# Moving the norm's sums and the first scalings of an MLP one loop step later

## The chip, the cores and the metric

The kernel runs on one core of one Trainium2 chip. The metric is the device time of one execution in microseconds; of several runs the median counts. Engines are named as in the profile: PE (matmuls), DVE (vector), ACT (activations), POOL (GpSimd), SP (the queue from which the DMAs are issued).

## The reference

Two layers on a sequence of 1024 tokens with 1024 features: a recurrent block, then chunked band attention, and behind each of them an MLP with its own RMS norm. Only the MLPs are touched by the change:

```python
def rmsnorm(x, g):
    xf = x.astype(jnp.float32)
    y = xf * lax.rsqrt(jnp.mean(xf * xf, axis=-1, keepdims=True) + EPS)
    return (y * g.astype(jnp.float32)).astype(x.dtype)

def sqrelu_mlp(x, w_up, w_down):
    return jnp.square(jax.nn.relu(x @ w_up)) @ w_down
...
        h = h + sqrelu_mlp(rmsnorm(h, mlp_norm[l]), w_up[l], w_down[l])
```

The factor of the norm is one number for each token. It is the same for all features, so it can be multiplied in after the product with `w_up`, and this is what the kernel does.

## The kernel before

Activations lie transposed: 128 features on the partitions, 512 tokens (a "half" h of the sequence) in the free dimension. Every fp32 operand is split in two fp32r tiles (`wh`, `wl` for weights, `h`, `l` for data: ACT makes the high part with a copy, DVE the low part with a subtraction), and one product of two blocks is three matmuls, high x high, high x low, low x high (lines 334 to 336).

`w_up` is multiplied by a 2x2 block scheme with seven products in place of eight. `mlp_up` runs 16 block pairs q. For each of them SP loads four weight blocks into `raw` tiles (A11, A12, A21, A22), POOL forms four sums of them (`up_sums`, lines 1044 to 1049), and seven splits are made by `wsplit` (ACT L1035, DVE L1036). Each `product` is 12 matmuls. In short, per q:

- z gets product 0 (bank "pj"), v gets product 1 ("sc"); c11 = z + v (ACT L1132, DVE L1133);
- y gets product 4 ("tp"), z gets product 5, w gets product 2 ("tp"), z gets product 6; c12 and c22 are sums of these (L1145 to L1152);
- `relu` scales c11, c12, c22 by the norm's factor R[0] or R[1] (DVE L1116) and squares them (ACT L1117);
- the `tail`, which is emitted one step later, behind the products 0 and 1 of q+1: product 3 goes into z, and c21 is `relu` of z (so that the bank of z is free only after that L1116); seven results go to DRAM (`hid`).

There are two "pj" banks, so that z of q+2 takes the bank of z of q. The first block pair (q = 0) is begun in `up_begin`, with its c11, c12, c22 in tiles of other pools; it ends with the squares of the last four result blocks and their addition to `norm.acc` (L1106, L1107) and with `c22 = z + c22` (L1108).

R comes from `o.r(h)`, that is `rneg`: the sum of squares `acc[h]` is split (`parts`: ACT L359 makes `ah`, DVE L361 makes `al`), summed over partitions by two matmuls with ones (`sums`: L365, L366), and from that ACT makes Ln (L393), Exp (L394) and a Square (L370), and DVE the two steps of a Newton correction (L371, L372). R[0] and R[1] are made once for each MLP.

`mlp_up` and `mlp_down` are recorded in plain program order, and the tile scheduler of the framework then puts the instructions of each engine in a fixed order of its own; the engines run in that order. What is emitted later has a lower priority there.

Of the kernel before, what the change touches and what calls it, by code (L numbers as in the profile page):

```python
# [13 lines left out]
ALU = mybir.AluOpType  # L14
# [143 lines left out]
def tile_yoco_rglru_chunk_attention(  # L158
# [72 lines left out]
    def bank(tag=None):  # L231
        if tag is None:
            tag = ("pj", "tp", "sc", "pj", "tp", "sc", "po", "sc")[ring[0] % 8]
            ring[0] += 1
        return ps1.tile([P, H2], F32, tag=tag, name=nm(tag), bufs=BANKS[tag])
# [6 lines left out]
    def dma(dst, src):  # L242
        ins = nc.sync.dma_start(dst, src)
        if early[0]:
            early[0] -= 1
            tc.keep_in_program_order(ins)
# [84 lines left out]
    def mm(ps, wp_, xp, start, stop, more=False):  # L331

        (wh, wl), (xh, xl) = wp_, xp
        pe.matmul(ps, lhsT=wh, rhs=xh, start=start, stop=False, skip_group_check=more)  # L334
        pe.matmul(ps, lhsT=wh, rhs=xl, start=False, stop=False, skip_group_check=more)  # L335
        pe.matmul(ps, lhsT=wl, rhs=xh, start=False, stop=stop, skip_group_check=more)  # L336
# [64 lines left out]
    R = [None, None]  # L401
# [631 lines left out]
    def wsplit(raw):  # L1033
        wh, wl = wr("wh"), wr("wl")
        act.activation(wh, raw, AF.Copy)  # L1035
        dve.tensor_tensor(wl, raw, wh.bitcast(F32), ALU.subtract)  # L1036
        return blocks4(wh), blocks4(wl)

    def up_weights(layer, q):
        raw = [wload(w_up[layer, q, x]) for x in range(4)]  # L1040
        return raw, (wsplit(raw[A11]), wsplit(raw[A12])), wsplit(raw[A22])
# [21 lines left out]
    def product(o, ps, n, w, start, depth=range(4)):  # L1063
        for i in depth:
            mm(
                ps, (w[0][:, i, :], w[1][:, i, :]), o.XT[n][i],
                start and i == 0, i == 3, not start and len(depth) == 4,
            )
# [42 lines left out]
    def mlp_up(o, layer, begun):  # L1111

        R = []

        def relu(out, src, h, op):
            dve.scalar_tensor_tensor(out, src, 0.0, R[h], op, ALU.mult)  # L1116
            act.activation(out, out, AF.Square)  # L1117

        (z, a22, c11, c12, c22), ahead = begun
        tail = None  # L1120
        for q in range(NQ + 1):
            if 0 < q < NQ:
                if q == 1:
                    raw, (a11, a12) = ahead
                    a22 = wsplit(raw[A22])
                else:
                    raw, (a11, a12), a22 = up_weights(layer, q)
                z, v = bank("pj"), bank("sc")
                product(o, z, 0, a11, True)
                product(o, v, 1, a12, True)  # L1130
                c11 = sf()
                act.activation(c11, z, AF.Copy)  # L1132
                dve.tensor_tensor(c11, v, c11, ALU.add)  # L1133
            if tail is not None:
                tail()
                tail = None
            if q == NQ:
                break
            if q:
                s1, s2 = up_sums(raw)  # L1140
                y = bank("tp")
                product(o, y, 4, s1, True)
                product(o, z, 5, s2, False)
                c12, c22 = sf(), sf()
                act.activation(c22, y, AF.Copy)  # L1145
                dve.tensor_tensor(c12, z, c22, ALU.add)
                s4, s3 = wsplit(raw[A12]), wsplit(raw[A11])
                w = bank("tp")
                product(o, w, 2, s4, True)
                dve.tensor_tensor(c12, w, c12, ALU.add)  # L1150
                product(o, z, 6, s3, False)
                dve.tensor_tensor(c22, z, c22, ALU.add)  # L1152
            else:
                R.extend((o.r(0), o.r(1)))
            relu(c11, c11, 0, ALU.max)
            relu(c12, c12, 1, ALU.max)
            relu(c22, c22, 1, ALU.min)

            def tail(q=q, z=z, a22=a22, c11=c11, c12=c12, c22=c22):
                product(o, z, 3, a22, False)  # L1160
                dma(hid[0, q], c11)
                dma(hid[2, q], c22)
                t1 = sf()
                dve.tensor_tensor(t1, c11, c12, ALU.subtract)
                dma(hid[4, q], t1)
                dve.tensor_tensor(c12, c22, c12, ALU.subtract)
                dma(hid[6, q], c12)
                t2 = sf()
                dve.scalar_tensor_tensor(t2, t1, -1.0, c22, ALU.mult, ALU.subtract)
                dma(hid[5, q], t2)  # L1170
                c21 = sf()
                relu(c21, z, 0, ALU.min)
                dma(hid[1, q], c21)
                t4 = sf()
                dve.scalar_tensor_tensor(t4, t2, -1.0, c21, ALU.mult, ALU.subtract)
                dma(hid[3, q], t4)
# [147 lines left out]
    X, R = o2.XS, o2.rr  # L1324
# [475 lines left out]
```

## Time and profile before

| | us |
|---|---|
| median of 3 runs | 2140.32 (2138.83 to 2141.16) |
| the profiled execution | 2141.76, of which its span is 2140.0 |
| PE busy | 2092.7 (98% of the span) |
| DVE busy | 1544.4 (72%) |
| ACT busy | 1106.4 (52%) |
| POOL busy | 577.2 (27%) |

A start time in the rows below is in us from the begin of the span. The first MLP's up stage starts near 340, the second's near 1535. "Busy" counts from start to end of an instruction, and instructions of one engine overlap a little: PE issues a 512 column matmul every 0.2275 us in full flow while one row lasts 0.39, and DVE and ACT issue every 0.60 and 0.53 us rows that last 0.68 and 0.62.

### The profile page before, as it was taken

What the parts mean: (1) busy time and instruction counts of PE and PEld (TensorE: products, weight loads), DVE (VectorE), ACT (ScalarE), POOL (GpSimd) and SP (SyncE); (2) the same over time, 40 slices, a digit from 0 to 9 for tenths busy, and PEclk for the clock granted to TensorE, in tenths of its full rate; (3) what the DMA queues carried; (4) which work ended last, traced back from release to release, by engine and by line L of the source; (5) the groups of instructions that cost most, each with busy time, mean ns of one, the idle gap of its engine ahead of it and who ended that gap; (6) DMA issues with size and microseconds to landing.
All of it is one profiled execution on the core that took longest, in us unless ns stands there. A gap on an engine that the chain in (4) does not pass through costs nothing.

```text
span 2140.0 us, 29346 instructions
## 1 busy us (share of the span) xinstructions
PE 2092.7 (98%) x9768; PEld 1732.8 (81%) x9768; DVE 1544.4 (72%) x2602; ACT 1106.4 (52%) x1965; POOL 577.2 (27%) x511
## 2 busy tenths in 40 slices
PE   7999899999999999999999999989999999999999
PEld 5788787888888888887888888878778888888887
DVE  7767768877777776747777877767787777777843
ACT  5777645444434544546666666764443444444631
POOL 0123202333310000127666666650133332000000
PEclk8999999999999999999999999999999999999999
DMA  4111334544469784534323332343364444987732
GB/s 139 35 50 50 107 116 153 182 158 153 149 231 314 240 259 131 161 121 109 86 75 97 91 91 83 87 151 123 103 215 148 155 156 170 332 262 242 244 109 94
DMA packets 174296, 319.21 MB, mean 149 GB/s; under 512 B 20544, under 2 KB 22592, under 8 KB 174144
## 3 DMA queue, kind: packets, MB, share of 16 engines
q1 hardware_dynamic: 174144, 317.33, 45.8%
q8 instruction: 77, 1.26, 0.2%
q14 instruction: 75, 0.61, 0.1%
HBM read 219.73 MB, written 78.64 MB: 139 GB/s over the span
## 4 chain that ended last, share of the span: by engine, by line
PE 86%; DVE 6%; ACT 3%; DMA 2%; issue 2%; SPq 1%; POOL 0%; DVEq 0%; POOLq 0%; ACTq 0%
PE pj L334 11%; PE pj L335 11%; PE pj L336 11%; PE tp L334 6%; PE tp L336 6%; PE tp L335 6%; PE sc L336 4%; PE sc L335 4%; PE sc L334 4%; PE p L335 4%; PE p L334 3%; PE p L336 3%; PE tp L1581 2%; PE po L1609 2%; PE po L1608 1%
## 5 line engine op out<-in xcount | busy, mean ns | idle before, releaser
L334 PE MATMUL pj<-h,wh 128*128 128x512 f32 x1198 | 481.5, 402 | 4.9 <-DVE s L1116 3.6
L335 PE MATMUL pj<-l,wh 128*128 128x512 f32 x1198 | 468.0, 391 | 0.7 <-POOL l L1634 0.7
L336 PE MATMUL pj<-h,wl 128*128 128x512 f32 x1198 | 467.9, 391 | 0.2
L1035 ACT ACTIVATE wh<-raw 128x512 fp32r<-128x512 f32 x349 | 219.1, 629 | 317.5 <-PE po L335 68.9
L1036 DVE TENSOR_TENSOR wl<-raw,wh 128x512 fp32r<-128x512 f32 x349 | 269.8, 775 | 100.3 <-ACT wh L1035 96.5
L336 PEld LDWEIGHTS pj<-h,wl 128*128 128x128 f32 x1198 | 225.2, 188 | 49.4 <-DVE wl L1036 1.0
L334 PEld LDWEIGHTS pj<-h,wh 128*128 128x128 f32 x1198 | 225.8, 189 | 48.5 <-DVE s L1116 4.4
L335 PEld LDWEIGHTS pj<-l,wh 128*128 128x128 f32 x1198 | 226.0, 189 | 38.8 <-POOL l L1634 1.4
L334 PE MATMUL tp<-h,wh 128*128 128x512 f32 x569 | 221.5, 389 | 0.0
L335 PE MATMUL tp<-l,wh 128*128 128x512 f32 x569 | 221.4, 389 | 0.0
L336 PE MATMUL tp<-h,wl 128*128 128x512 f32 x569 | 221.4, 389 | 0.0
L348 DVE TENSOR_TENSOR l<-raw,h 128x512 fp32r<-128x512 f32 x224 | 153.6, 692 | 30.1 <-ACT h L347 28.6
L347 ACT ACTIVATE h<-raw 128x512 fp32r<-128x512 f32 x224 | 137.5, 620 | 56.9 <-DMA raw<-hid 34.1
L335 PE MATMUL sc<-l,wh 128*128 128x512 f32 x425 | 165.8, 390 | 0.0
L336 PE MATMUL sc<-h,wl 128*128 128x512 f32 x425 | 165.7, 390 | 0.0
L334 PE MATMUL sc<-h,wh 128*128 128x512 f32 x425 | 165.4, 390 | 0.0
L334 PE MATMUL p<-h,wh 128*128 128x512 f32 x384 | 153.0, 398 | 11.3 <-ACT h L589 6.4
L1117 ACT ACTIVATE s<-s 128x512 f32<-128x512 f32 x125 | 78.4, 629 | 164.6 <-DVE s L1116 164.6
L1044 POOL TENSOR_TENSOR raw<-raw,raw 128x512 f32<-128x512 f32 x30 | 49.7, 1657 | 405.3 <-DVE wl L1036 398.3
L335 PE MATMUL p<-l,wh 128*128 128x512 f32 x384 | 152.5, 397 | 4.9 <-DVE l L592 2.4
L336 PE MATMUL p<-h,wl 128*128 128x512 f32 x384 | 151.3, 394 | 0.0
L334 PEld LDWEIGHTS tp<-h,wh 128*128 128x128 f32 x569 | 106.8, 188 | 22.4 <-ACT h L1632 0.3
(276 smaller groups left out, 4149.9 us busy)
## 6 DMA issues: line engine op xcount, KB each, us to landing
raw<-hid SPq DMA_DIRECT2D x224, 256.0 KB, 3.6
hid<-s SPq DMA_DIRECT2D x221, 256.0 KB, 2.1
raw<-in_w_down SPq DMA_DIRECT2D x192, 256.0 KB, 3.5
raw<-in_w_up SPq DMA_DIRECT2D x128, 256.0 KB, 2.6
s<-in_w_down SPq DMA_DIRECT2D x64, 256.0 KB, 4.3
raw<-in_w_in SPq DMA_DIRECT2D x32, 256.0 KB, 2.7
raw<-in_w_kv SPq DMA_DIRECT2D x32, 256.0 KB, 3.3
od<-ev SPq DMA_DIRECT2D x48, 128.0 KB, 2.2
```

The lines of the kernel that those rows point to most:

```text
L334: pe.matmul(ps, lhsT=wh, rhs=xh, start=start, stop=False, skip_group_check=more)
L335: pe.matmul(ps, lhsT=wh, rhs=xl, start=False, stop=False, skip_group_check=more)
L336: pe.matmul(ps, lhsT=wl, rhs=xh, start=False, stop=stop, skip_group_check=more)
L347: act.activation(h, src, AF.Copy)
L348: dve.tensor_tensor(l, src, h.bitcast(F32), ALU.subtract)
L1035: act.activation(wh, raw, AF.Copy)
L1036: dve.tensor_tensor(wl, raw, wh.bitcast(F32), ALU.subtract)
L1044: pool.tensor_tensor(raw[A11], raw[A11], raw[A21], ALU.add)
L1117: act.activation(out, out, AF.Square)
L1581: pe.transpose(pt[:, g * P : (g + 1) * P], sc[:, (kb - kb0) * P : (kb - kb0 + 1) * P], ident)
L1608: pe.matmul(out, lhsT=st, rhs=ph[:, off : off + wid], start=x == 0 and y == 0, stop=False)
L1609: pe.matmul(out, lhsT=st, rhs=pl[:, off : off + wid], start=False, stop=y == final)
```

## The change

`R.extend((o.r(0), o.r(1)))` and the three `relu` calls on c11, c12 and c22 go from the body of the loop into `tail`, behind its product 3. They are thus emitted one step later: behind the products 0 and 1 of the next q, its c11, and product 3 of the own q. For q = 0 the whole making of R moves with them. No instruction is added or removed on any engine.

```diff
                 product(o, z, 6, s3, False)
                 dve.tensor_tensor(c22, z, c22, ALU.add)
-            else:
-                R.extend((o.r(0), o.r(1)))
-            relu(c11, c11, 0, ALU.max)
-            relu(c12, c12, 1, ALU.max)
-            relu(c22, c22, 1, ALU.min)
 
             def tail(q=q, z=z, a22=a22, c11=c11, c12=c12, c22=c22):
                 product(o, z, 3, a22, False)
+                if not R:
+                    R.extend((o.r(0), o.r(1)))
+                relu(c11, c11, 0, ALU.max)
+                relu(c12, c12, 1, ALU.max)
+                relu(c22, c22, 1, ALU.min)
                 dma(hid[0, q], c11)
```

The order in which the scheduler puts the instructions differs at the head of each of the two up stages only: on PE over some 120 rows, on DVE and ACT over some 45. From the middle of the third block pair on, and everywhere else in the program, the rows stand on every engine as before. Three places matter.

**Place 1, DVE behind L1108** in the first MLP. `al` is the low part of the sum of squares, `wl` with raw_2491, raw_2489, raw_2487, raw_2485 the low parts of q = 1's blocks (A22 plain, then A21+A22, A22 with its sums, A12 with its sums, A11+A21). Before:

```order
L1108 TENSOR_TENSOR raw_2529<-pj_2455,raw_2529 128x512
L361 TENSOR_TENSOR al_2627<-acc_2313,ah_2625 128x512
L1036 TENSOR_TENSOR wl_2659<-raw_2491,wh_2658 128x512
L1036 TENSOR_TENSOR wl_2723<-raw_2489,wh_2722 128x512
L1036 TENSOR_TENSOR wl_2728<-raw_2491,wh_2727 128x512
L1036 TENSOR_TENSOR wl_2762<-raw_2487,wh_2761 128x512
L371 SCALAR_TENSOR_TENSOR s_2634<-po_2624,s_2634 128x512
L361 TENSOR_TENSOR al_2641<-acc_2315,ah_2639 128x512
L372 SCALAR_TENSOR_TENSOR rneg_2631<-s_2634,rneg_2631 128x512
```

Now:

```order
L1108 TENSOR_TENSOR raw_2529<-pj_2455,raw_2529 128x512
L1036 TENSOR_TENSOR wl_2625<-raw_2491,wh_2624 128x512
L361 TENSOR_TENSOR al_2672<-acc_2313,ah_2670 128x512
L1036 TENSOR_TENSOR wl_2723<-raw_2489,wh_2722 128x512
L1133 TENSOR_TENSOR s_2654<-sc_2629,s_2654 128x512
L1036 TENSOR_TENSOR wl_2728<-raw_2491,wh_2727 128x512
L1036 TENSOR_TENSOR wl_2762<-raw_2487,wh_2761 128x512
L1036 TENSOR_TENSOR wl_2766<-raw_2485,wh_2765 128x512
L1036 TENSOR_TENSOR wl_2805<-raw_2796,wh_2804 128x512
L1036 TENSOR_TENSOR wl_2809<-raw_2798,wh_2808 128x512
L371 SCALAR_TENSOR_TENSOR s_2679<-po_2669,s_2679 128x512
L361 TENSOR_TENSOR al_2686<-acc_2315,ah_2684 128x512
```

The split of A22 now stands ahead of `al`; c11 of q = 1 and three more splits (the last two of q = 2) stand ahead of the Newton step L371.

**Place 2, the sums of the second half** in the first MLP, on ACT and on PE. On ACT, `ah` with acc_2315 is the second half's. Before:

```order
L359 ACTIVATE ah_2625<-acc_2313 128x512
L1035 ACTIVATE wh_2722<-raw_2489 128x512
L393 ACTIVATE rneg_2631<-po_2624,eps 128x512
L1035 ACTIVATE wh_2727<-raw_2491 128x512
L394 ACTIVATE rneg_2631<-rneg_2631 128x512
L1035 ACTIVATE wh_2761<-raw_2487 128x512
L370 ACTIVATE s_2634<-rneg_2631 128x512
L359 ACTIVATE ah_2639<-acc_2315 128x512
```

Now:

```order
L359 ACTIVATE ah_2670<-acc_2313 128x512
L1035 ACTIVATE wh_2722<-raw_2489 128x512
L1035 ACTIVATE wh_2727<-raw_2491 128x512
L1035 ACTIVATE wh_2761<-raw_2487 128x512
L1035 ACTIVATE wh_2765<-raw_2485 128x512
L1035 ACTIVATE wh_2804<-raw_2796 128x512
L1035 ACTIVATE wh_2808<-raw_2798 128x512
L393 ACTIVATE rneg_2676<-po_2669,eps 128x512
L394 ACTIVATE rneg_2676<-rneg_2676 128x512
L370 ACTIVATE s_2679<-rneg_2676 128x512
L359 ACTIVATE ah_2684<-acc_2315 128x512
```

Three more splits now stand ahead of the second `ah`. On PE, the first half's sums (po) stood among the last ten matmuls of q = 1's product 1 and now stand behind product 3 of q = 0 (pj_2455); then comes product 5 of q = 1 (pj_2628). The second half's sums (tp_2683) stand behind that and one matmul of q = 2:

```order
L335 MATMUL pj_2628<-l_2524,wh_2727 128x512
L336 MATMUL pj_2628<-h_2523,wl_2728 128x512
L334 MATMUL sc_2817<-h_1994,wh_2808 128x512
L365 MATMUL tp_2683<-ah_2684,onesr 128x512
L334 MATMUL tp_2732<-h_2031,wh_2722 128x512
L335 MATMUL tp_2732<-l_2032,wh_2722 128x512
L336 MATMUL tp_2732<-h_2031,wl_2723 128x512
L366 MATMUL tp_2683<-al_2686,onesr 128x512
```

Before, the second half's L365 stood right behind product 3 of q = 0, 22 rows behind L365 of the first half; now it is 15 behind it, and product 5 has come ahead of the products 4 and 2 of q = 1.

**Place 3, DVE ahead of c21 of q = 0** in the first MLP, L1116 on pj_2455; the first matmul of z of q = 2 waits for that row. Before:

```order
L371 SCALAR_TENSOR_TENSOR s_2648<-tp_2638,s_2648 128x512
L1133 TENSOR_TENSOR s_2688<-sc_2663,s_2688 128x512
L372 SCALAR_TENSOR_TENSOR rneg_2645<-s_2648,rneg_2645 128x512
L1116 SCALAR_TENSOR_TENSOR s_2688<-s_2688,rneg_2631 128x512
L1116 SCALAR_TENSOR_TENSOR raw_2528<-raw_2528,rneg_2645 128x512
L1116 SCALAR_TENSOR_TENSOR raw_2529<-raw_2529,rneg_2645 128x512
L1036 TENSOR_TENSOR wl_2819<-raw_2808,wh_2818 128x512
L1164 TENSOR_TENSOR s_2705<-raw_2527,raw_2528 128x512
L1036 TENSOR_TENSOR wl_2883<-raw_2806,wh_2882 128x512
L1166 TENSOR_TENSOR raw_2528<-raw_2529,raw_2528 128x512
L1169 SCALAR_TENSOR_TENSOR s_2710<-s_2705,raw_2529 128x512
L1116 SCALAR_TENSOR_TENSOR s_2713<-pj_2455,rneg_2631 128x512
```

Now:

```order
L1116 SCALAR_TENSOR_TENSOR s_2654<-s_2654,rneg_2676 128x512
L1036 TENSOR_TENSOR wl_2883<-raw_2800,wh_2882 128x512
L371 SCALAR_TENSOR_TENSOR s_2693<-tp_2683,s_2693 128x512
L372 SCALAR_TENSOR_TENSOR rneg_2690<-s_2693,rneg_2690 128x512
L1036 TENSOR_TENSOR wl_2888<-raw_2802,wh_2887 128x512
L1116 SCALAR_TENSOR_TENSOR raw_2528<-raw_2528,rneg_2690 128x512
L1116 SCALAR_TENSOR_TENSOR raw_2529<-raw_2529,rneg_2690 128x512
L1036 TENSOR_TENSOR wl_2922<-raw_2798,wh_2921 128x512
L1164 TENSOR_TENSOR s_2705<-raw_2527,raw_2528 128x512
L1166 TENSOR_TENSOR raw_2528<-raw_2529,raw_2528 128x512
L1169 SCALAR_TENSOR_TENSOR s_2710<-s_2705,raw_2529 128x512
L1116 SCALAR_TENSOR_TENSOR s_2713<-pj_2455,rneg_2676 128x512
```

Between L1108 and this L1116 stood 23 DVE rows and stand 25 now: two more splits of q = 2 (wl_2888, wl_2922) have come ahead of it. On PE, four more matmuls of q = 2's product 4 have come ahead of the z that waits for it. In the second MLP the same places are changed in nearly the same way, there with two matmuls in place of four.

## Rows read from the trace of the kernel before

**Rows 1.** The page: the span; busy time of each engine; the chain that ended last, by engine.

```profile
span 2140.0 us, 29346 instructions
PE 2092.7 (98%) x9768; PEld 1732.8 (81%) x9768; DVE 1544.4 (72%) x2602; ACT 1106.4 (52%) x1965; POOL 577.2 (27%) x511
...
PE 86%; DVE 6%; ACT 3%; DMA 2%; issue 2%; SPq 1%; POOL 0%; DVEq 0%; POOLq 0%; ACTq 0%
```

**Rows 2.** Busy time of each engine in stretches at the head of the up stage of the first MLP (340 to 380) and of the second (1550 to 1570), with one from the steady part (400 to 440). Columns: stretch, its length, then for each engine busy us and, in brackets, instructions; then the granted clock of PE as a share of full speed, DMA share, GB/s.

```profile
340.00:350.00 10.00, 7.91 (x32) 5.86 (x31) 9.87 (x13) 5.42 (x11) 3.50 (x3) 0.95 0.01 2
350.00:360.00 10.00, 10.00 (x40) 8.07 (x40) 7.29 (x12) 8.30 (x15) 4.77 (x4) 0.88 0.55 180
360.00:370.00 10.00, 8.25 (x37) 6.52 (x36) 10.00 (x13) 4.52 (x9) 4.08 (x3) 1.00 0.77 265
370.00:380.00 10.00, 9.75 (x43) 7.61 (x42) 9.85 (x15) 5.16 (x10) 3.11 (x3) 1.00 0.83 272
400.00:440.00 40.00, 40.00 (x178) 33.13 (x177) 29.35 (x40) 15.60 (x27) 14.79 (x10) 1.00 0.45 151
...
1550.00:1560.00 10.00, 10.00 (x46) 8.29 (x45) 9.35 (x13) 6.29 (x12) 5.51 (x4) 1.00 0.90 292
1560.00:1570.00 10.00, 8.18 (x35) 6.14 (x35) 9.86 (x15) 4.65 (x8) 3.76 (x3) 1.00 0.75 256
```

**Rows 3.** The timeline of PE in the first MLP. Columns: start, duration, engine, line, operation, out<-in, shape, count; in brackets the idle time before the row and what ended it.

```profile
345.54 0.39 PE L334 MATMUL sc<-h,wh 128*128 128x512 f32 x1
347.94 0.50 PE L365 MATMUL po<-ah,onesr 128*128 128x512 f32 x1 [2.01 <-ACT ah L359]
...
350.13 0.63 PE L334 MATMUL sc<-h,wh 128*128 128x512 f32 x1
350.56 0.63 PE L335 MATMUL sc<-l,wh 128*128 128x512 f32 x1
...
354.67 0.39 PE L365 MATMUL tp<-ah,onesr 128*128 128x512 f32 x1
...
366.94 0.39 PE L335 MATMUL tp<-l,wh 128*128 128x512 f32 x1
369.07 0.50 PE L334 MATMUL pj<-h,wh 128*128 128x512 f32 x1 [1.75 <-DVE s L1116]
...
376.07 0.39 PE L336 MATMUL tp<-h,wl 128*128 128x512 f32 x1
376.71 0.50 PE L334 MATMUL pj<-h,wh 128*128 128x512 f32 x1 [0.25 <-DVE s L1152]
```

**Rows 4.** The same view of PE in the second MLP, the rows with idle time before them.

```profile
1541.33 0.50 PE L365 MATMUL po<-ah,onesr 128*128 128x512 f32 x1 [2.02 <-ACT ah L359]
...
1547.91 0.50 PE L365 MATMUL tp<-ah,onesr 128*128 128x512 f32 x1 [1.26 <-ACT ah L359]
...
1562.49 0.50 PE L334 MATMUL pj<-h,wh 128*128 128x512 f32 x1 [1.82 <-DVE s L1116]
```

**Rows 5.** The timeline of DVE in the first MLP (the last row: the second MLP's L1108), same columns.

```profile
347.74 0.68 DVE L1108 TENSOR_TENSOR raw<-pj,raw 128x512 f32<-128x512 f32 x1
348.35 0.67 DVE L361 TENSOR_TENSOR al<-acc,ah 128x512 fp32r<-128x512 f32 x1
...
352.06 1.22 DVE L1036 TENSOR_TENSOR wl<-raw,wh 128x512 fp32r<-128x512 f32 x1 [1.84 <-ACT wh L1035]
...
359.06 0.69 DVE L371 SCALAR_TENSOR_TENSOR s<-tp,s 128x512 f32<-128x512 f32 x1 [0.72 <-ACT s L370]
359.67 0.68 DVE L1133 TENSOR_TENSOR s<-sc,s 128x512 f32<-128x512 f32 x1
...
364.34 1.78 DVE L1036 TENSOR_TENSOR wl<-raw,wh 128x512 fp32r<-128x512 f32 x1
366.04 1.78 DVE L1166 TENSOR_TENSOR raw<-raw,raw 128x512 f32<-128x512 f32 x1
...
368.34 0.68 DVE L1116 SCALAR_TENSOR_TENSOR s<-pj,rneg 128x512 f32<-128x512 f32 x1
...
1541.14 0.68 DVE L1108 TENSOR_TENSOR s<-pj,s 128x512 f32<-128x512 f32 x1
```

**Rows 6.** The timeline of POOL in the first MLP: its sums for q = 1 (from 349) and for q = 2 (from 359), same columns.

```profile
349.79 1.57 POOL L1047 TENSOR_TENSOR raw<-raw,raw 128x512 f32<-128x512 f32 x1 [3.72 <-DVE wl L1036]
351.44 1.29 POOL L1049 TENSOR_TENSOR raw<-raw,raw 128x512 f32<-128x512 f32 x1
...
359.56 1.29 POOL L1045 TENSOR_TENSOR raw<-raw,raw 128x512 f32<-128x512 f32 x1
363.95 1.61 POOL L1047 TENSOR_TENSOR raw<-raw,raw 128x512 f32<-128x512 f32 x1 [3.10 <-DVE wl L1036]
365.64 1.62 POOL L1049 TENSOR_TENSOR raw<-raw,raw 128x512 f32<-128x512 f32 x1
```

**Rows 7.** The timeline of ACT in the first MLP, two rows that follow each other, same columns.

```profile
353.31 0.62 ACT L370 ACTIVATE s<-rneg 128x512 f32<-128x512 f32 x1
353.83 0.62 ACT L359 ACTIVATE ah<-acc 128x512 fp32r<-128x512 f32 x1
```

**Rows 8.** The queue of SP in the first MLP (three loads of q = 2's blocks, of which the first, A12, is issued at the row's start), and the page's row on these loads: size and median us from issue to landing.

```profile
350.25 4.23 SPq L243 DMA_DIRECT2D raw<-in_w_up  x3
...
raw<-in_w_up SPq DMA_DIRECT2D x128, 256.0 KB, 2.6
```

## The prediction

> **What bounds the kernel now.** I read the page first: PE is busy for 2092.7 of 2140.0 us and holds 86% of the chain that ended last [rows 1]. So only time in which PE stands still, or runs slowly, can be won. The order says that instructions move at the head of the two up stages and nowhere else, so I read the busy time by stretches there. In the steady part PE has no gap (40.00 of 40.00) with DVE at 29.35; at the head of the first MLP PE loses 2.1, 1.75 and 0.25 us in three stretches, its clock is at 0.88 in one, and DVE is the full engine: 9.87, 10.00 and 9.85 of 10 us [rows 2]. The timeline of PE names the gaps. First MLP: 2.01 us for ACT's `ah`, 1.75 for DVE's L1116 (c21 of q = 0, which frees the bank for z of q = 2) and 0.25 for L1152 [rows 3]. Second MLP: 2.02 and 1.26 for `ah`, 1.82 for L1116 [rows 4]. That is 9.1 us, and all the change can win, but for some matmuls at half clock (0.43 us apart where 0.2275 is usual, rows of 0.63 us near 350) [rows 3].
>
> **Three prices from the rows.** PE issues every 0.2275 us (54 matmuls from 354.67 to 366.94 [rows 3]); 0.10 more behind a gap. DVE issues every 0.60 (359.06 to 359.67), a row ends 0.68 after its start [rows 5]. ACT issues every 0.53, a row lasts 0.62 [rows 7]. What waits for another engine starts 0.03 to 0.06 behind its end (L1116 ends at 369.02, PE starts at 369.07 [rows 3, 5]). Then there is a fourth price, which a median would hide: two DVE rows lasted 1.78 us, and each ends 0.56 us behind a POOL row that was running when it started (POOL ends 365.56, DVE 366.12; POOL 367.26, DVE 367.82) [rows 5, 6]. The split at 352.06 took 1.22 in the same way: POOL ends at 352.73. POOL in turn lasts 1.29 alone and 1.6 where it met DVE [rows 6]. So the two take turns. A DVE row that reads PSUM is spared: L1133 at 359.67 lasted 0.68 with POOL's row from 359.56 running [rows 5, 6].
>
> [...]
>
> **The change, part by part.** No instruction is added or removed, no DMA either. What the change moves is the place of each at the head of both stages.
>
> *First gap of PE.* Behind the row of 345.54 eight more matmuls of product 1 follow now; the sums are no longer among them. PE is done with these at 347.59 and comes to product 3 of q = 0, which writes on the z that L1108 reads. L1108 ends at 347.74 + 0.68 = 348.42 [rows 5], unchanged, so PE goes on at 348.47: a gap of 0.9 where 2.17 (347.94 less 345.77, when the next one was due) was lost. The first half's sums, 12 matmuls later at 351.30, find `ah` and `al` made. Gain so far 1.3.
>
> *Splits of q = 1.* The split of A22 goes to 348.35, POOL may start L1047 0.6 us sooner, asks at 349.19, gets its turn at 349.47 and ends at 350.76 (before 351.36 [rows 6]). The split of A21+A22 on DVE, at 349.55, now comes behind it: it ends at 351.31, 1.1 us later than before. L1049 runs from 351.16 to 352.45, the next split ends behind it at 353.00. PE needs that one at 352.21 (third matmul of product 5): gap 0.84, new.
>
> *Second half's sums.* ACT makes six splits ahead of them now: the fourth sum's from 352.49, then one more of q = 1 and two of q = 2 every 0.53, L393 at 354.6, L394, L370, and `ah` from 356.25 to 356.87. Before it stood at 353.83 [rows 7]. PE is there at 355.65 and starts L365 at 356.93: gap 1.27, new in the first MLP; in the second 1.26 was there already [rows 4]. PE has now lost 3.0 where it had lost 2.17 and some half-clock matmuls.
>
> *c21 of q = 0.* This row decides where both orders meet, and it is DVE's. From L1108 to it there were 24 steps and are 26. Before: 347.74 + 24 x 0.60 = 362.14; it started at 368.34 [rows 5], so 6.2 us were waits. Now: 363.34 plus waits, which I follow row by row. For POOL: the split of A21+A22 1.08, the next 0.49, L372 behind L1045 of q = 2 1.10 (that POOL row runs to 358.8, since its blocks come at about 356.5: issued at 353.9, as soon as the split at 353.15 is done, and 2.6 to land [rows 8]), c11 of q = 1 behind L1047 1.08, a split behind L1049 1.09: 4.84. For ACT: 0.23 and 0.80. Sum 5.87, start 369.2, end 369.92, and PE goes on at 369.97. It was ready at 367.5 (42 matmuls behind L366 at 357.94), a gap of 2.5. Before, the same matmul's place was four earlier: 369.07 + 4 x 0.2275 = 369.98. Gain 0.0: what PE wins at the first gap it loses at the others, since DVE is full and got two more rows ahead of c21.
>
> *Second MLP.* The same walk from L1108 at 1541.14 [rows 5]: 26 x 0.60 = 15.6, waits for POOL 1.08, 0.49, 0.79, 0.48, 1.08, 1.08 and for ACT 0.22, 0.29, 0.08, sum 5.59; c21 starts at 1562.33 and PE at 1563.06. Before: 1562.49 [rows 4], with two matmuls more ahead now 1562.95. Loss 0.1. The gaps of PE there become 0.9, 0.8, 1.3, 0.8, 1.65, in place of 2.02, 1.26, 1.82.
>
> *Behind it.* The gap of 0.41 us at 376.71 (idle 0.25; due at 376.30, 0.2275 behind 376.07 [rows 3]) came since L1152 stood behind an L1164 that waited for POOL. Now L1152 stands ahead of it: gain 0.4. In the second MLP I take the same.
>
> *The later scalings* (q from 1 on) are hidden by a PE with no gap and a DVE at 73% [rows 2], and the order there is unchanged: 0. The moved `hid` DMAs wait in SP behind later rows; they are needed a whole stage later: 0.
>
> **Sum.** 0.0 + 0.4 - 0.1 + 0.4 = 0.7 us gained. The profiled span becomes 2139.3 (its execution 2141.76 becomes 2141.1), the median 2140.32 becomes **2139.6**.
>
> **Bounds of the unknown.** The waits for POOL are in no row for the new order; if all went (4.84 and 5.0), PE's own readiness would set: 367.5 and 1561.4, gain 2.5 + 1.65 + 0.7 = 4.8 in all. Each hit row more costs 1.1 to 1.3. The block A12 of q = 2 is issued at 351.3, not 350.25, and lands 2.6 later [rows 8], 353.9, when ACT wants it at 354.1: a late one moves `ah` and c21 by as much, in the first MLP alone. A half clock behind the 2.5 us gap, as near 350 behind the one of 2.01, would cost nine matmuls at 0.2 more, 1.8 us. I take the middle, as the rows of DVE near 364 are nearest to it.
>
> **Rivals.**
> - *POOL's turns fall better* (price 0 to 4.8 us): for it, whether a row meets POOL's hangs on a tenth of a microsecond (POOL gets its turn at 349.47, the split would start at 349.55); against it, PE's own new gaps of 0.84 and 1.27 stay. Time 2136 to 2138, with all of it 2135.5.
> - *All gaps close*: 9.1 us [rows 3, 4], 2131.2. Against it DVE's 10.00 of 10 us [rows 2]: it can't bring c21 sooner with two more rows ahead.
> - *Slower: more rows of the scaling chain meet POOL's sums.* Place: DVE between L371 and c21; price 1.1 to 1.29 for each hit row. It decides from four more hits over both stages (0.7 + 4.3 = 5.0 us lost against the walk), 2144.6. For it: DVE and POOL take turns when both are ready, and fourteen rows there read SBUF twice. Against it: POOL has but four sums for a block pair, and nearly all of them already meet a row in the walk.
>
> **How the numbers follow.** From no change a measurement of this kernel can tell about 0.2%, 4.3 us: 2136.0 and 2144.6. Walk as above, within 2.5 us: 0.70. POOL's turns better: 0.14, half of it under 2136.0. All gaps close, or most: 0.04. Slower chain: 0.12, of it 0.07 over 2144.6. So faster 0.11, same 0.82, slower 0.07. The range leaves out the closed gaps and the ends of both neighbours: 2135.5 to 2143.5.
>
> **What would show it.** PE: the first gap ends at L1108 and is near 0.9; new ones stand before a product-5 matmul (for L1036) and before L365 on tp (for ACT's L359); the largest stands before z of q = 2, 2 to 2.5 us, still put down to L1116. DVE: busy 9.8 or more in 340 to 380, with four or five rows of 1.2 to 1.8 us from 349 to 364. Wrong I would be if that last gap is under 1 us, or c21 starts before 367 or behind 371, or if PE shows gaps behind 385.

## The result and the profile after

The changed kernel takes 2144.62 us (median of 20 runs, 2141.81 to 2149.78) where the kernel before takes 2140.49 (20 runs, 2138.03 to 2143.11): ratio 1.0018, 95% interval 1.0012 to 1.0024. It is slower, by 4.1 us; the prediction said 2139.6 and no change. The profiled execution of the changed kernel took 2142.94 us, its span is 2141.2. A second measurement (E9 below) gave 2144.72 beside 2141.22. The profiled spans of before and after (2140.0 and 2141.2) differ by less than the medians: between the heads of the two MLPs, from the steady part of the first up stage on, the profiled execution of before takes the longest of the thirteen of this text (1118.3 us between the same two matmuls, 1115.5 in the change, 1115.0 to 1118.0 in all others), though the order there is that of the change. So the heads are compared below by distances inside them.

The page, for [rows 1]: span, busy time, chain.

```profile
span 2141.2 us, 29345 instructions
...
PE 2092.3 (98%) x9768; PEld 1732.6 (81%) x9768; DVE 1552.6 (73%) x2602; ACT 1107.6 (52%) x1965; POOL 579.4 (27%) x511
...
PE 84%; DVE 7%; ACT 3%; DMA 2%; issue 2%; POOL 1%; SPq 0%; DVEq 0%; ACTq 0%; POOLq 0%
```

PE does the same work, and DVE has one per cent more of the chain. The timeline of PE with every row that has idle time of 0.5 us or more before it, and the rows right ahead of the last gaps, for [rows 3, 4] (first MLP, then second):

```profile
347.63 0.50 PE L334 MATMUL pj<-h,wh 128*128 128x512 f32 x1 [0.75 <-DVE raw L1108]
...
352.23 0.50 PE L336 MATMUL pj<-h,wl 128*128 128x512 f32 x1 [0.68 <-DVE wl L1036]
...
356.32 0.50 PE L365 MATMUL tp<-ah,onesr 128*128 128x512 f32 x1 [1.30 <-ACT ah L359]
...
369.78 0.50 PE L334 MATMUL pj<-h,wh 128*128 128x512 f32 x1 [2.73 <-DVE s L1116]
...
385.74 0.39 PE L336 MATMUL tp<-h,wl 128*128 128x512 f32 x1
387.13 0.50 PE L334 MATMUL pj<-h,wh 128*128 128x512 f32 x1 [0.99 <-DVE s L1146]
...
1541.28 0.50 PE L334 MATMUL pj<-h,wh 128*128 128x512 f32 x1 [0.74 <-DVE s L1108]
...
1545.88 0.50 PE L336 MATMUL pj<-h,wl 128*128 128x512 f32 x1 [0.68 <-DVE wl L1036]
...
1550.35 0.50 PE L365 MATMUL tp<-ah,onesr 128*128 128x512 f32 x1 [1.22 <-ACT ah L359]
1551.91 0.50 PE L366 MATMUL tp<-al,onesr 128*128 128x512 f32 x1 [0.60 <-DVE al L361]
...
1562.89 0.50 PE L334 MATMUL pj<-h,wh 128*128 128x512 f32 x1 [1.83 <-DVE s L1116]
...
1577.78 0.39 PE L336 MATMUL tp<-h,wl 128*128 128x512 f32 x1
1578.72 0.50 PE L334 MATMUL pj<-h,wh 128*128 128x512 f32 x1 [0.55 <-DVE s L1146]
```

The gaps up to z of q = 2 stand where the walk has them. Those at 387.13 and 1578.72, before product 6 of q = 2, are new, and no step of the prediction has them. Nor does it have the half clock behind the gap of 2.73 in its sum. The stretches, for [rows 2]:

```profile
360.00:370.00 10.00, 7.27 (x33) 5.72 (x32) 9.86 (x13) 4.93 (x9) 2.75 (x2) 1.00 0.61 209
370.00:380.00 10.00, 10.00 (x37) 7.84 (x37) 6.54 (x11) 3.89 (x7) 2.09 (x2) 0.83 0.75 270
```

From 370 to 380 the granted clock is 0.83 and PE gets 37 matmuls done where it got 43 before with a gap: seven rows of 0.63 us, from 370.42 to 372.98, stand 0.43 us apart where 0.2275 is usual, and from 370.85 to 373.41 the granted clock is 0.50, the half clock of this text. DVE, full before (9.85), is busy for 6.54 us of the 10.

Where the time goes is read from DVE's L1108, from its L1152 (the last sum of a block pair; from one to the next takes 19.04 us in the steady part of both kernels), and from PE's product 6 of q = 2, the matmul of the late gap, which has the same number of matmuls ahead of it in both kernels. What stands ahead of L1108 is the same in both kernels and still differs by some 3 us between profiled executions (L1108 starts at 346.90 to 349.75 in the thirteen of this text), so only distances from it count. The timeline of DVE before:

```profile
375.98 0.68 DVE L1152 TENSOR_TENSOR s<-pj,s 128x512 f32<-128x512 f32 x1
...
380.18 1.78 DVE L1169 SCALAR_TENSOR_TENSOR s<-s,s 128x512 f32<-128x512 f32 x1
...
384.19 0.68 DVE L1146 TENSOR_TENSOR s<-pj,s 128x512 f32<-128x512 f32 x1
...
387.97 0.69 DVE L1152 TENSOR_TENSOR s<-pj,s 128x512 f32<-128x512 f32 x1 [0.71 <-PE pj L336]
...
1569.00 0.68 DVE L1152 TENSOR_TENSOR s<-pj,s 128x512 f32<-128x512 f32 x1
...
1581.03 0.69 DVE L1152 TENSOR_TENSOR s<-pj,s 128x512 f32<-128x512 f32 x1 [0.73 <-PE pj L336]
```

PE before, in either MLP the matmul ahead of product 6 of q = 2 and the first of it, without a gap:

```profile
384.77 0.39 PE L336 MATMUL tp<-h,wl 128*128 128x512 f32 x1
385.00 0.41 PE L334 MATMUL pj<-h,wh 128*128 128x512 f32 x1
...
1577.84 0.39 PE L336 MATMUL tp<-h,wl 128*128 128x512 f32 x1
1578.07 0.40 PE L334 MATMUL pj<-h,wh 128*128 128x512 f32 x1
```

And DVE after:

```profile
346.90 0.68 DVE L1108 TENSOR_TENSOR raw<-pj,raw 128x512 f32<-128x512 f32 x1
...
376.46 0.69 DVE L1152 TENSOR_TENSOR s<-pj,s 128x512 f32<-128x512 f32 x1 [3.29 <-PE pj L336]
377.07 0.68 DVE L1036 TENSOR_TENSOR wl<-raw,wh 128x512 fp32r<-128x512 f32 x1
...
378.26 0.69 DVE L1133 TENSOR_TENSOR s<-sc,s 128x512 f32<-128x512 f32 x1
378.87 1.20 DVE L1164 TENSOR_TENSOR s<-s,s 128x512 f32<-128x512 f32 x1
379.99 1.78 DVE L1036 TENSOR_TENSOR wl<-raw,wh 128x512 fp32r<-128x512 f32 x1
...
384.69 1.78 DVE L1175 SCALAR_TENSOR_TENSOR s<-s,s 128x512 f32<-128x512 f32 x1
386.39 0.68 DVE L1146 TENSOR_TENSOR s<-pj,s 128x512 f32<-128x512 f32 x1
...
390.48 0.68 DVE L1152 TENSOR_TENSOR s<-pj,s 128x512 f32<-128x512 f32 x1
...
1540.55 0.68 DVE L1108 TENSOR_TENSOR s<-pj,s 128x512 f32<-128x512 f32 x1
...
1568.06 0.69 DVE L1152 TENSOR_TENSOR s<-pj,s 128x512 f32<-128x512 f32 x1 [1.78 <-PE pj L336]
...
1582.07 0.68 DVE L1152 TENSOR_TENSOR s<-pj,s 128x512 f32<-128x512 f32 x1
```

With the two L1108 of before from [rows 5], the distances are:

| us | before | after | E9 (the same kernel) |
|---|---|---|---|
| first MLP: L1108 to L1152 of q = 1 | 28.24 | 29.56 | 28.02 |
| L1152 of q = 1 to that of q = 2 | 11.99 | 14.02 | 14.02 |
| L1152 of q = 2 to that of q = 3 | 19.04 | 18.74 | 18.75 |
| L1108 to the matmul ahead of product 6 of q = 2 | 37.03 | 38.84 | 37.29 |
| L1108 to product 6 of q = 2 | 37.26 | 40.23 | 38.69 |
| second MLP: L1108 to L1152 of q = 1 | 27.86 | 27.51 | 29.08 |
| L1152 of q = 1 to that of q = 2 | 12.03 | 14.01 | 14.00 |
| L1152 of q = 2 to that of q = 3 | 19.04 | 18.74 | 18.74 |
| L1108 to the matmul ahead of product 6 of q = 2 | 36.70 | 37.23 | 38.80 |
| L1108 to product 6 of q = 2 | 36.93 | 38.17 | 39.73 |

From L1108 to L1152 of q = 3 the change takes 3.05 and 1.33 us longer, E9 1.52 and 2.89: 4.4 in both runs, and from there on each pair takes 19.04 us as before. PE's own rows divide these 4.4 us in three. Up to the matmul ahead of product 6 of q = 2, where no half clock is, PE is 0.26 us later than before in the first MLP (E9) and 0.53 in the second (the change): 0.8 over both. In each of the two runs one MLP, not the same one, is 1.55 us later than that: the one in which PE ran at half clock. And the gap before product 6 costs 1.17 and 0.71, with 0.1 more behind it each time: 2.05 over both. (DVE's L1152 of q = 1 comes 0.2 to 0.35 us sooner than before where no half clock is, but that is not PE's gain: before, PE's product was done when a full DVE came to that row, and now DVE waits for PE there.)

Between the first L1152 and L1146 of q = 2, for which PE waits at 387.13, DVE ran 10 rows before (8.21 us: 10 x 0.60, and 2.2 of rows that ended late) and runs 12 now (9.93: 12 x 0.60, and 2.7 of rows that ended late). One split (q = 3's A11, L1036 at 377.07), c11 of q = 2 (L1133) and a sum (L1164) stood ahead of L1152 before and stand behind it now; one split (of q = 3's A21+A22) went from ahead of this L1146 to behind it. And POOL's sums of q = 3, which can't start before the split of A11, come 4.5 to 5.4 us later than before, counted from L1108. Two of them before:

```profile
374.20 1.30 POOL L1044 TENSOR_TENSOR raw<-raw,raw 128x512 f32<-128x512 f32 x1 [6.94 <-DMA raw<-in_w_up]
...
379.80 1.61 POOL L1047 TENSOR_TENSOR raw<-raw,raw 128x512 f32<-128x512 f32 x1 [2.61 <-DVE wl L1036]
```

And after:

```profile
377.83 1.69 POOL L1044 TENSOR_TENSOR raw<-raw,raw 128x512 f32<-128x512 f32 x1 [14.99 <-DVE wl L1036]
...
384.31 1.61 POOL L1047 TENSOR_TENSOR raw<-raw,raw 128x512 f32<-128x512 f32 x1 [3.10 <-DVE wl L1036]
```

The second runs till 385.92 and holds DVE's L1175 for 1.78 us, till 386.47, right ahead of the L1146 that PE waits for.

### The profile page after: what moved, and what is told of

The parts are those of the page before. It is cut to its first block, busy times and chain, and to the rows that moved or that the text cites. A ratio compares the mean times of both kernels' runs of the same rounds, so it can differ in the third digit from the quotient of the medians.

```text
span 2141.2 us, 29345 instructions
## 1 busy us (share of the span) xinstructions
PE 2092.3 (98%) x9768; PEld 1732.6 (81%) x9768; DVE 1552.6 (73%) x2602; ACT 1107.6 (52%) x1965; POOL 579.4 (27%) x511
## 3 DMA queue, kind: packets, MB, share of 16 engines
q8 instruction: 77, 1.26, 0.2%
## 4 chain that ended last, share of the span: by engine, by line
PE 84%; DVE 7%; ACT 3%; DMA 2%; issue 2%; POOL 1%; SPq 0%; DVEq 0%; ACTq 0%; POOLq 0%
PE pj L334 11%; PE pj L336 11%; PE pj L335 11%; PE tp L334 5%; PE tp L336 5%; PE tp L335 5%; PE sc L335 4%; PE sc L336 4%; PE sc L334 4%; PE p L335 4%; PE p L336 3%; PE p L334 3%; PE tp L1581 2%; PE po L1609 1%; PE po L1608 1%
## 5 line engine op out<-in xcount | busy, mean ns | idle before, releaser
L1036 DVE TENSOR_TENSOR wl<-raw,wh 128x512 fp32r<-128x512 f32 x349 | 276.9, 796 | 96.4 <-ACT wh L1035 92.6
L1044 POOL TENSOR_TENSOR raw<-raw,raw 128x512 f32<-128x512 f32 x30 | 49.7, 1657 | 412.4 <-DVE wl L1036 397.7
L294 POOL TENSOR_TENSOR raw<-raw,vec 128x512 f32<-128x512 f32 x48 | 54.2, 1129 | 263.2 <-DMA raw<-in_w_kv 259.6
```

The source lines that it names most:

```text
L294: pool.tensor_tensor(raw, raw, gains, ALU.mult)
L1044: pool.tensor_tensor(raw[A11], raw[A11], raw[A21], ALU.add)
```

## The experiments

Edits are shown against the changed kernel, "..." marks lines left out. "Less before" is the median minus that of the kernel before in the same comparison; the ratio goes by all runs and not by the two medians, so that its sign can differ (E10). "PE idle" adds the idle times of 0.2 us and more in PE's timeline over both heads (L1108 to product 6 of q = 2); the last column counts PE's rows of 0.6 us and more that follow one another there, at half clock. Both are of the profiled execution.

| | us | less before | ratio, 95% interval | PE idle | half clock |
|---|---|---|---|---|---|
| before | 2140.49 | | | 9.1 | 7 |
| the change | 2144.62 | +4.1 | 1.0018 (1.0012 to 1.0024) | 12.1 | 7 |
| E1, q = 1 to 15 only | 2141.42 | +0.5 | 1.0002 (0.9994 to 1.0011) | 9.7 | 7 |
| E2, split in own tiles | 2149.69 | +8.7 | 1.0039 (1.0026 to 1.0051) | 14.4 | 13 |
| E3, c21 first | 2147.47 | +6.5 | 1.0030 (1.0018 to 1.0042) | 14.0 | 0 |
| E4, all behind L1152 | 2136.11 | -4.8 | 0.9975 (0.9965 to 0.9985) | 5.5 | 0 |
| E5, scalings only | 2142.27 | +1.3 | 1.0010 (1.0000 to 1.0019) | 11.1 | 0 |
| E6, no sums of q = 2 | 2137.15 | -3.8 | 0.9984 (0.9976 to 0.9993) | 6.8 | 0 |
| E7, no sums of q = 3 | 2142.25 | +1.3 | 1.0006 (0.9998 to 1.0015) | 10.3 | 0 |
| E8, q = 0 only | 2145.53 | +4.6 | 1.0025 (1.0015 to 1.0035) | 13.3 | 7 |
| E9, the change again | 2144.72 | +3.5 | 1.0017 (1.0008 to 1.0026) | 12.1 | 7 |
| E10, R kept, rest later | 2140.77 | -0.4 | 1.0004 (0.9995 to 1.0013) | 9.9 | 0 |
| E11, all behind L1146 | 2139.47 | -1.8 | 0.9990 (0.9981 to 0.9999) | 8.1 | 19 |

The times follow PE's idle time in the heads: the two differences from before agree within 1.7 us, but for E2 (3.4).

**Which part does it: E1, E5, E8.** E1:

```diff
                 dve.tensor_tensor(c22, z, c22, ALU.add)
+            else:
+                R.extend((o.r(0), o.r(1)))
+                relu(c11, c11, 0, ALU.max)
...
                 product(o, z, 3, a22, False)
-                if not R:
-                    R.extend((o.r(0), o.r(1)))
-                relu(c11, c11, 0, ALU.max)
...
+                if q:
+                    relu(c11, c11, 0, ALU.max)
...
```

> The changed kernel, but the first block pair (q = 0) is handled as in the kernel before: R and its three scalings stand at their old place, and only the scalings of q = 1 to 15 go into the tail. Theory 'late split' (the loss comes from the rows of q = 0: they put L1152 of q = 1, which waits for PE, ahead of the first split of q = 3 on DVE, and POOL's sums of q = 3 then fall ahead of L1146 of q = 2): here the split of q = 3 stands ahead of L1152 as before, PE's gaps are those of before (2.0 and 1.75 us in the first MLP) and there is none behind 385; 2140.5 us within 1. Rival 'later scalings' (every pair's scaling one step later makes DVE late in each step): PE has gaps before product 6 of q = 2 and of later pairs; 2142.5 to 2144.6.

Measured: 2141.42, and no gap behind 385. The gaps are not quite those of before: that at c21 is 0.83 and 0.84 us, 0.62 and 0.71 come ahead of it for a split, and in the second MLP one of 1.40 for L1152 is new. In sum they are 9.7 us where before had 9.1: the scalings of q = 1 to 15 cost nothing that can be told.

E5 leaves R at its old place (an `else: R.extend(...)` in the loop) and moves all three scalings, those of q = 0 too.

> Only the three scalings go into the tail; the making of R is emitted at its old place, in the loop's body. On all five engines the instructions come out in the order of the changed kernel, row for row. So the time has to be that of the changed kernel, 2144.6 within 1, with the same gaps of PE (2.7 and 1.0 in the first MLP, 1.8 and 0.6 in the second). A theory by which R's own lines do the harm would want 2140.5. It is also a second profile of that order: 'half clock follows the long gap' expects the nine matmuls behind the gap of 2.7 us to be 0.43 apart again.

The second sentence is wrong: the order on all five engines is that of E1, row for row, and so is the result, 2142.27 with the gaps of E1. So the place where the scalings are emitted does not matter even for q = 0; it is R's place that does. In this second profile of one order the first MLP has no half clock, and a gap of 1.25 us ahead of the second half's sums that E1 lacks.

E8 is the other half: R and q = 0's scalings in the tail (`if not R:` before all four lines), those of q = 1 on at their old place.

> Only q = 0 is changed: R and its three scalings are made in the tail, the scalings of q = 1 to 15 stand at their old place. If the loss comes from the first pair alone: 2144.6 within 1.5, with the gap of 2.7 ahead of z of q = 2 and one before product 6 of q = 2. If it takes both parts together: 2140.5 to 2142.5, no gap behind 385.

Measured: 2145.53, with gaps of 2.73 and 1.85 ahead of z of q = 2 and of 1.59 and 1.11 before product 6 of q = 2. So the loss comes from q = 0 alone. The late gaps are 0.6 us longer than the change's; DVE has 13 rows between L1152 and L1146 there, one more.

**What the late gap waits for: E7, E2.** E7:

```diff
-                s1, s2 = up_sums(raw)
+                s1, s2 = (wsplit(raw[A21]), wsplit(raw[A22])) if q == 3 else up_sums(raw)
```

It leaves out POOL's four sums of q = 3; the splits take the blocks as loaded.

> The changed kernel without POOL's four sums of q = 3 in the same way; the order on PE, DVE and ACT stays as it is. In the changed kernel these sums hold DVE for 2.75 us between L1146 of q = 1 and L1146 of q = 2 in each MLP. Theory 'POOL's turns hold DVE': L1146 of q = 2 comes 2 us sooner, the gaps of PE before product 6 of q = 2 (0.99 and 0.55) go, the others stay: 2144.6 - 1.5 = 2143.1. Rival 'idle DVE' (the 3.3 us in which DVE waits for PE behind L1152 of q = 1 set it): the gaps stay within 0.3, 2144.6.

Measured: 2142.25, and both late gaps are gone. What is left of the loss is what PE loses ahead of product 6: L1152 of q = 3 stands 0.25 and 0.48 us later behind L1108 than before. DVE in the first MLP:

```profile
377.80 0.69 DVE L1152 TENSOR_TENSOR s<-pj,s 128x512 f32<-128x512 f32 x1 [1.77 <-PE pj L336]
...
384.42 0.69 DVE L1175 SCALAR_TENSOR_TENSOR s<-s,s 128x512 f32<-128x512 f32 x1
385.02 0.69 DVE L1146 TENSOR_TENSOR s<-pj,s 128x512 f32<-128x512 f32 x1
```

The same 12 rows take 7.22 us, 12 x 0.60: all 2.7 us of late rows were POOL's turns (in the change no row there has idle time before it, so it is not that splits wait for the sums). L1175 took 1.78 us with a sum running and 0.69 without. The trace of before has more of such rows: of those that start while one of POOL's sums (L1044 to L1049) runs, the 85 with two SBUF tiles as inputs last 1.00 to 1.78 us, the 57 that read one of PE's banks 0.68 or 0.69. The rival falls with it: DVE still stands idle ahead of L1152 here, and there is no late gap. E9 says the same from the other side: idle for 1.73 us ahead of L1152 in one MLP and for 3.33 in the other, with the same late gaps of 1.01 and 0.55 as the change (3.29 and 1.78).

E2 tried to have the split of q = 3 ahead of L1152, as before:

```diff
-    def wsplit(raw):
-        wh, wl = wr("wh"), wr("wl")
+    def wsplit(raw, own=False):
+        wh, wl = (gr("wh"), gr("wl")) if own else (wr("wh"), wr("wl"))
...
-        return raw, (wsplit(raw[A11]), wsplit(raw[A12])), wsplit(raw[A22])
+        return raw, (wsplit(raw[A11], q == 3), wsplit(raw[A12])), wsplit(raw[A22])
```

> The changed kernel, but the split of q = 3's block A11 takes two tiles of another pool, so that it waits for no matmul that frees a tile of the weights' pool, and stands 8 rows sooner on DVE (ahead of L1152 of q = 1, one row ahead of c21 of q = 0). Theory 'late split': DVE is not idle ahead of L1152, POOL's L1044 of q = 3 starts near 373 in place of 377.8, and the gaps of PE before product 6 of q = 2 (0.99 and 0.55) go; that gives back the 2.0 us lost between the first two L1152 of each MLP, and costs 0.6 at c21 for the row more: 2144.6 - 4.0 + 1.2 = 2141.8. Rival 'half clock alone' (the later gaps only follow from PE's 1.8 us at half clock, which made L1152 late): they stay, and with c21 later the time is 2144.6 to 2145.8.

Measured: 2149.69, worse by 5 us than the change, and both theories missed it. POOL's sum started sooner (370.86), but the splits went ahead not only of L1152 but also of c21 of q = 0 and of L1146 of q = 1, which have 31 rows ahead in place of 29 in the first MLP, and DVE is full there (9.97 of 10 us in 360 to 370): gaps of 1.45 and 1.20 at these two, still 0.92 at L1146 of q = 2; in the second MLP 3.42 us at c21, with half clock behind it. It doesn't show what it was made for, since it moved more than the one split. With one row more ahead of c21, PE got on there 0.4 and 2.3 us later behind L1108 than in the change.

**The large gap ahead of z of q = 2: E6, E3.** E6 is E7 with `q == 2`, so it leaves out POOL's sums of q = 2.

> The changed kernel without POOL's four sums of q = 2 (the splits that read them take the blocks as loaded, so that part of w_up's scheme is left out for this pair); the order on PE, DVE and ACT stays as it is. Theory 'POOL's turns hold DVE': the three DVE rows of 1.78 us from 356.99 to 361.60 fall to 0.68, c21 of q = 0 comes some 3.3 us sooner (1 us less where L371 then waits for ACT), and the gap ahead of z of q = 2 (2.73 and 1.83) shrinks to 0 to 0.7; with it goes the half clock behind it (1.8 a stage): 2144.6 - 4 - 1.8 = 2138.8, 2137 to 2140. Rival (c21 waits for ACT's chain to R, not for DVE's turn): the gap stays over 1.5 us and the time over 2143.

Measured: 2137.15. The gap ahead of z of q = 2 is gone in both MLPs, and there is no half clock; DVE's rows of 1.78 us near 360 lasted 0.69. So POOL's turns make c21 late, as the walk of the prediction had it. The gap at L1146 of q = 2 stays (0.96 and 0.51): it has its own sums, those of q = 3.

E3 moves three lines up in the tail, and nothing else:

```diff
                     R.extend((o.r(0), o.r(1)))
+                c21 = sf()
+                relu(c21, z, 0, ALU.min)
+                dma(hid[1, q], c21)
                 relu(c11, c11, 0, ALU.max)
```

> The changed kernel, but in the tail c21 is scaled first, ahead of c11, c12 and c22 (on DVE it stands 9 rows sooner, and L1146 of q = 1 where it was). By the rows of the changed kernel DVE comes to c21 at 363.3 and PE waits some 1.5 us for it, then some 1.5 for L1146 of q = 1 before product 6: the gap of 2.73 becomes two of about 1.5. Theory 'half clock follows the long gap': with no gap over 2 us the matmuls behind it run at 0.2275, 1.8 us are saved in each stage where they didn't; and the split of q = 3 stands ahead of L1152 again, so the gaps of 0.99 and 0.55 go: 2144.6 - 1.8 to 3.6 - 1.5 + 0.6 = 2140.1 to 2141.9. Rival (the half clock has nothing to do with that gap, and DVE's load alone makes the later ones): 2144 to 2145.

Measured: 2147.47, a miss by 6 us. The first part came as expected in the first MLP, one gap became two:

```profile
366.24 0.50 PE L334 MATMUL pj<-h,wh 128*128 128x512 f32 x1 [1.51 <-DVE s L1116]
...
373.77 0.50 PE L334 MATMUL pj<-h,wh 128*128 128x512 f32 x1 [1.12 <-DVE s L1146]
```

There was no half clock. But the late gaps did not go, they grew to 1.68 and 1.22; 0.78 came in the second MLP for L1152; and each up stage got a gap at its end for L1152 of the last pair (1.26 at 641.67, 1.63 at 1835.79). What a line that stands first does to all other pairs I had not followed.

**Which rows stand ahead: E4, E10, E11.** E4 takes the change a step further:

```diff
             if tail is not None:
-                tail()
+                rest = tail()
...
                 dve.tensor_tensor(c22, z, c22, ALU.add)
+            if rest is not None:
+                rest()
...
                 product(o, z, 3, a22, False)
...
+                def rest():
+                    if not R:
+                        R.extend((o.r(0), o.r(1)))
+                    c21 = sf()
+                    relu(c21, z, 0, ALU.min)
+                    dma(hid[1, q], c21)
+                    relu(c11, c11, 0, ALU.max)
...
+                return rest
```

All else that stood in the tail follows in `rest()` in its old order.

> One step further than the change: R, c21 and all that the tail does behind its product 3 is emitted behind the next pair's last sum (L1152). On DVE L1146 of q = 1 then stands at row 11 behind L1108 (29 in the changed kernel), c21 of q = 0 at row 23 (26), and PE has all of q = 1's products before it needs c21. Theory 'order of rows' (what counts is which rows stand ahead of those for which PE waits, not the load): a gap of some 0.75 for L1108 and one of some 0.7 for a split stay in each MLP, the others go: 2140.5 - 9.1 + 2 x 1.5 = 2134.4, below 2137 in any case. Rival 'full DVE' (DVE has no room near 350 to 385, so what is put off there makes gaps later): gaps of 2 to 4 us in each MLP between 370 and 400; 2139 to 2142.

Measured: 2136.11, faster than both kernels. The gaps of PE that are left in the first MLP are 0.76 us for L1108, 0.25 for L1132 and 0.76 and 0.82 for L1148, which is L1146 here (the second MLP has 0.76, 1.11, 0.24 and 0.83). The first of L1148:

```profile
361.84 0.50 PE L334 MATMUL pj<-h,wh 128*128 128x512 f32 x1 [0.76 <-DVE s L1148]
```

DVE runs the same 2602 rows, in another order, so a full DVE as such was not the limit. The gaps of 1.8 to 2.7 us are gone; PE has all of q = 1 to do before it needs c21 of q = 0; the expectation had missed the gaps at L1148.

E10 leaves R and c21 in the tail and puts only the rest behind L1152.

> Between the change and the kernel of E4: R and c21 stay in the tail where the change puts R, and only the rest of the tail (the scalings of c11, c12, c22, the sums t1, c12, t2, t4 and their DMAs) goes behind the next pair's last sum. On DVE L1146 of q = 1 then stands 19 rows behind L1108 (29 in the changed kernel, 11 in E4's), c21 of q = 0 17 (26, 23), and R's sums are where the change puts them. If the rows ahead of those two set the time, this lies between the two kernels: the gap ahead of z of q = 2 goes, one of 2 to 2.7 us ahead of product 6 of q = 1 comes (PE is there at 362.5, L1146 ends at 365.2 by the changed kernel's rows), none at product 6 of q = 2: 2140 to 2142. If only R's place counted (the theory 'R's sums hold PE and ACT'), it would be as slow as the change: 2144 to 2145.

Measured: 2140.77, in the range, the same as before: gaps of 1.73 and 1.48 at product 6 of q = 1, none at c21 and none at q = 2. R stands where the change puts it, the gaps of its own sums (1.29 and 1.21) are those of the change, and yet the two large gaps are gone. So most of the harm that the place of R does comes through the rows that it draws with it, not by its own matmuls.

E11 is E4 with `rest()` behind L1146 in place of L1152.

> As E4, but R, c21 and the rest are emitted behind the next pair's first sum (L1146) and not behind its last (L1152). L1146 of q = 1 stands at row 11 on DVE as in E4, c21 of q = 0 at row 21 (23 in E4), R's sums some 50 matmuls sooner on PE. By the theory 'rows ahead of those PE waits for' it is within 1.5 us of E4, 2135 to 2137.5; if R's place counted, it would lie in the middle between E4 and the change, near 2140.

Measured: 2139.47, a miss, and near the 2140 that went with R's place. But the rows put it elsewhere. Of R's own sums there is one gap of 1.21 us, in the first MLP. L1146 of q = 1 has 11 rows ahead as in E4, but PE has gaps of 2.51 and 2.89 us there:

```profile
360.37 0.50 PE L334 MATMUL pj<-h,wh 128*128 128x512 f32 x1 [2.51 <-DVE s L1148]
```

L1148 comes 11.86 us behind L1108, in E4 11.93. It is PE that is there sooner: product 2 of q = 1, twelve matmuls, stands behind that wait here and ahead of it in E4, with four of q = 2 in its place (8 x 0.2275 = 1.8 us, and the gaps are 1.75 and 1.78 longer). Its one profile, with 19 rows at half clock, may not be typical: the two heads take 1.1 us longer in it than before, while the median is 1.8 less. The row's place on DVE is half of the answer; what PE has to do ahead of its wait is the other half.

**The half clock: E9.**

> The changed kernel once more, beside the next two on one chip: 2144.6 within 1, 4 us over the kernel before. In its profile: gaps of PE ahead of z of q = 2 of some 2.7 us in the first MLP and 1.8 in the second, and before product 6 of q = 2 of some 1.0 and 0.6. 'Half clock follows the long gap' expects the matmuls behind the first to be 0.43 apart and those behind the second not.

Measured: 2144.72. The gaps agree with those of the change to 0.02 us (L1108 and product 6 of q = 2 are shown too, for the table above), the half clock does not stay in its place:

```profile
348.30 0.68 DVE L1108 TENSOR_TENSOR raw<-pj,raw 128x512 f32<-128x512 f32 x1
...
371.20 0.50 PE L334 MATMUL pj<-h,wh 128*128 128x512 f32 x1 [2.71 <-DVE s L1116]
...
386.99 0.50 PE L334 MATMUL pj<-h,wh 128*128 128x512 f32 x1 [1.01 <-DVE s L1146]
...
1541.12 0.68 DVE L1108 TENSOR_TENSOR s<-pj,s 128x512 f32<-128x512 f32 x1
...
1563.48 0.50 PE L334 MATMUL pj<-h,wh 128*128 128x512 f32 x1 [1.84 <-DVE s L1116]
...
1565.12 0.63 PE L334 MATMUL pj<-h,wh 128*128 128x512 f32 x1
...
1580.85 0.50 PE L334 MATMUL pj<-h,wh 128*128 128x512 f32 x1 [0.55 <-DVE s L1146]
```

Its stretches:

```profile
370.00:375.00 5.00, 3.80 (x17) 3.12 (x18) 4.42 (x7) 1.50 (x3) 0.00 (x0) 1.00 0.99 355
...
1565.00:1570.00 5.00, 5.00 (x16) 3.88 (x16) 1.80 (x3) 0.67 (x2) 0.00 (x0) 0.68 0.96 306
```

Behind the gap of 2.71 us the clock stays at 1.00, behind that of 1.84 it falls to 0.68 in the stretch. So "half clock follows the long gap" does not hold as expected.

## Why the prediction was wrong

- *First gap, splits of q = 1, second half's sums*: predicted 0.9, 0.84 and 1.27 us from due to start; 0.75, 0.68 and 1.30 idle, which is 0.9, 0.84 and 1.46 from due. Right.
- *c21 of q = 0*: right in kind, short in size. Predicted 21.5 us behind L1108 (369.2 less 347.74), measured 22.14 (369.04 less 346.90): the waits for POOL and ACT ahead of it came to 6.5 us in place of 5.87. In E6, without the sums of q = 2, it is 19.44, so that 2.7 of the waits are turns of these sums. PE went on at z of q = 2 22.88 us behind L1108, before 21.33 with four matmuls fewer done (0.9 us): 0.65 lost where the walk had 0.0. In the second MLP the five gaps 0.9, 0.8, 1.3, 0.8, 1.65 came as 0.74, 0.68, 1.22, 0.60, 1.83 of idle time, and 0.55 was lost there (22.34, before 21.35 with two matmuls fewer) where the walk had 0.1.
- *L1152 of q = 1* (0.4 gained in each MLP): right in the first, where 0.4 of the 0.65 lost at c21 is won back ahead of product 6. In the second the kernel before had no such gap [rows 4], so there was nothing to gain, and the 0.4 taken for it was without a row.
- **"Behind it" and "The later scalings"** are where it failed most. The walk ended at L1152 of q = 1, and behind it stood "the order there is unchanged: 0". The order was not unchanged: by the front it differs up to the middle of the third pair, and from L1152 of q = 1 to L1146 of q = 2 it has 12 rows on DVE in place of 10, with POOL's sums of q = 3 some 5 us later among them. Measured: PE loses 1.26 and 0.80 us there, 2.05 in all, where 0 was in the sum. Rows that no longer stood ahead of L1152 did not vanish; they stood behind it, ahead of the next wait.
- **The half clock** was a bound of 1.8 us and not in the sum. It is in all three profiled executions that have the gaps of 2.7 and 1.8 us, in one MLP (the change, E8 and E9), and costs 1.5 to 1.6 us (29.56 less 28.02, 29.08 less 27.51). Before it is there as well [rows 3], but near 350, ahead of waits that hide it: E1 and E5 have one order, E1 with half clock near 350 and E5 without, and E5 waits 1.25 us for `ah` where E1 does not wait at all. With the change it falls behind the last long wait. There L1152 hangs on PE, L1146 on L1152 and PE on L1146, so nothing takes it up: the late gaps are the same with and without it.
- Sum: 0.7 gained was predicted, and 4.4 lost by the rows (medians 4.1 and 3.5). The 5.1 between them are 1.1 at c21, 0.4 at the second MLP's L1152, 2.05 behind L1152 and 1.55 of half clock.
- *The rival "Slower"* gave 2144.6, the right time from the wrong place: it looked for more rows that meet POOL's sums between L371 and c21. The late gap is behind c21, and POOL's turns are 0.5 of the 1.7 us by which L1146 is later there; the two rows are 1.2.
- *What would show it* named gaps behind 385 as the sign of being wrong. They came, at 387.13 and, as far behind L1108, at 1578.72.

What makes half clock come in one MLP and not in the other stays open: no run here sets it. Which of the waits ahead of c21 the walk had too short is not tried by a run. Of E7's 1.3 us over before, the heads show 0.7; the rest is open.

## What to carry to other kernels

When a change reorders a full engine, follow the walk until the two orders meet on every engine, not to the first row that stands level: what has been pushed behind one wait is due before the next. Count the rows from each row that waits for the bounding engine to the next row for which that engine waits, and the neighbour's sums that they meet (a row took 1.78 us beside one of POOL's here, 0.69 without). To shorten such a head, put off the rows whose results are needed last behind the sums for which the bounding engine waits first (E4), and see that the bounding engine still has work ahead of its wait (E11).

## What the runs showed of the hardware

- One order, run twice, with gaps of PE equal to 0.02 us: once the clock fell behind an idle time of 2.73 us (0.83 in 370 to 380, 0.50 in 370.85 to 373.41) and not behind 1.83 (1.00 in 1560 to 1570), once behind 1.84 (0.68 in the stretch) and not behind 2.71 (1.00). Elsewhere it fell behind 3.42 (E2, 13 rows of 0.61 to 0.80 us, 0.89 in 1570 to 1590), 2.89 (E11, seven rows of 0.63 to 0.79) and 2.00 (E1, seven of 0.63, 0.91 in 340 to 350), and not behind 2.02 and 2.03 (E5, no row of 0.6 or more). The idle time right before it does not settle it, and no run here shows what does.
- Without POOL's sums, twelve DVE rows on end, nine of them with two SBUF operands, stand 0.60 us apart (E7); with them, two of the rows take 1.78 and one 1.20.
